# Attention 0 of a two-layer encoder: which engine makes the cosine products, the gated head outputs and the squares of the softmax sums

## The chip, the cores and the metric

The kernel runs on one core of a Trainium2 chip. Its five engines have a queue of instructions each and take them strictly in order: TensorE (PE in the profile, with its weight loads as PEld), VectorE (DVE), ScalarE (ACT), GpSimd (POOL) and SyncE (SP), which here only issues DMAs. They wait for each other through semaphores. The metric is the device time of one execution in microseconds; before the change the median of three runs is 1395.75 us (1395.17 to 1396.02).

Two memories matter. Tensors that work is done on lie in SBUF. Matmul results lie in PSUM, in eight banks of 128x512 fp32. A tile of PSUM is a bank here, or two for the scores.

## The reference, cut to what matters

Layer 0 is a differential attention with 8 heads of two 64-wide query/key components and 128-wide values, over 1024 positions; layer 1 is another attention that the change leaves alone.

```python
def _rope(x, positions):
    ...
    out = jnp.concatenate([x1 * cos - x2 * sin, x2 * cos + x1 * sin], axis=-1)

def _diff_attention(h, positions, w_in, ...):
    proj = h @ w_in
    q, k, v, z = jnp.split(proj, ...)
    q, k = _rope(q), _rope(k)
    ...
    def block(qb):
        sc = jnp.einsum('bqhcd,bkhcd->bhcqk', qb, k) * scale
        p = jax.nn.softmax(sc, axis=-1)
        p = p[:, :, 0] - lam * p[:, :, 1]
        return jnp.einsum('bhqk,bkhd->bqhd', p, v)
    ...
    o = _rmsnorm(o, subln_g) * (1.0 - lambda_init)
    o = o.reshape(b, s, DA_WIDTH) * jax.nn.silu(z)
    return o @ w_out
```

## The kernel before

The whole kernel is one straight program without loops on the chip; a framework resolves every dependency to semaphores and decides the order of each engine's queue when the program is built. `tc.keep_in_program_order` (through `in_turn`) and `tc.issue_after` (through `behind`) pin some instructions of the code to an order or behind another one.

A product in full precision is made of three matmuls on pairs of a high and a low part (`mm3`, lines 173 to 175). Making such a pair takes a cast on ScalarE (the high part, names that end in `h`) and a subtraction on VectorE or GpSimd (the low part, names that end in `l`).

**Attention 0** runs over heads 0 to 7, and per head over eight query tiles of 128 rows (`attn0`, `q_tile`). A query tile goes like this. For each of the two components c: four matmuls make the scores `s` (line 866, 128x1024, two banks; there are two such tiles), VectorE takes the row maximum `nm` (line 412), ScalarE the exponential `e` and its row sum (line 414). Then VectorE computes the ratio of the sums (`z`, lines 872 and 873) and combines the two components in one instruction (`e<-s,z,e`, line 874), which also sets the second score tile free. The combined tile is turned by eight transposes in two halves (`tr`, line 395; one bank); ScalarE makes the high part `pth` out of each half (line 397), VectorE the low part `ptl` (line 398), and only then is the one `tr` bank free for the next half. Every second query tile, matmuls with the values go into the bank `pv` (`Tail.pv`); after four query tiles, a half, the head's output 128x512 is complete there.

**Between these**, TensorE works on the stream (`stream0`): strips of k, q and the gate z of the next heads, 24 matmuls for each half of a strip, into the two `acc` banks (tables FILL0 and FILL7 say how many steps stand in which gap of a query tile). A finished half of a k or q strip goes to `rope`: ScalarE copies the bank to `rp_raw` (line 331 for k, 333 for q with its scale), four DMAs fetch the rotated rows into `rp_sw`, the cosine product `rp_r = rp_raw * cosT` is made (line 336), `rot` makes the sine product and adds it (lines 341 and 343, GpSimd), and `stack_k` / `stack_q` make the pairs `ks`, `qa` and `qb` for the scores: casts on ScalarE (356, 357, 364, 365), subtractions on GpSimd (358, 359, 366, 367), and DMAs for q. For head 0 VectorE does the cosine product, for heads 1 to 7 GpSimd (`eng`). `rp_raw`, `rp_sw` and `rp_r` share six buffers (tag `rp`).

**At the end of a half** `close` calls `head_out` and `subln`. `head_out` reads the `pv` bank twice on ScalarE: the squares `osq` (line 931) and `o`, scaled by the per-row constant `g8` (line 932). `subln` multiplies `o` by the gate `gz` on GpSimd (line 938); for the very last half (`late0`) VectorE does this (line 940). `rest`, some steps later, sums the squares with eight small matmuls into `ssq` (an `acc` bank, line 945) and makes the factor of each position out of `ssq` and the softmax sum `zz`: four VectorE instructions on 128x4 (lines 948 to 951), the power on GpSimd (`rq_y`, line 169) and a product with the guard `sl_f` (line 953). After a round trip through HBM that spreads the factor, `o` is scaled (line 908) and stored.

Of the kernel before, what the change touches and what calls it, by code (L numbers as in the profile page):

```python
# [15 lines left out]
AF = mybir.ActivationFunctionType  # L16
ALU = mybir.AluOpType
# [4 lines left out]
P = 128  # L22
# [5 lines left out]
NH = 8  # L28
QL = 384
KVL = 256  # L30
EPS = 1e-6
# [38 lines left out]
GUARD = 2.0 ** 40  # L70
FMAX = 3.4028e38
LAM0 = 0.8 - 0.6 * math.exp(-0.3 * 0)
SC0 = 64 ** -0.5
# [8 lines left out]
def trunk(ctx: ExitStack, tc: tile.TileContext, A, out):  # L82
    nc = tc.nc
    SP, PE, V, S, G = nc.sync, nc.tensor, nc.vector, nc.scalar, nc.gpsimd

    def pool(stack, name, bufs=1, side="left", space=None):
        kw = dict(name=name, bufs=bufs, reuse_waits="tile")
        if space is not None:
            kw["space"] = space
            if space == DRAM:  # L90
                kw.pop("reuse_waits")
        else:
            kw["side"] = side
        return stack.enter_context(tc.tile_pool(**kw))
# [49 lines left out]
    cosT = const.tile([P, T], F32, name="cosT")  # L144
# [14 lines left out]
    g8 = const.tile([P, 1], F32, name="g8")  # L159
# [20 lines left out]
    def behind(eng):  # L180

        return tc.issue_after(mk[eng]) if eng in mk else nullcontext()

    def in_turn(ins):

        return tc.keep_in_program_order(ins) if mk else ins
# [134 lines left out]
                self.count += 1  # L321
                side.tick()

    def rope(rp, acc, half, scale, eng=G, add=V):

        cs = slice(half * HF, half * HF + HF)
        raw = rp.tile([P, HF], F32, name="rp_raw", tag="rp", bufs=6)
        sw = rp.tile([P, HF], F32, name="rp_sw", tag="rp", bufs=6)
        r = rp.tile([P, HF], F32, name="rp_r", tag="rp", bufs=6)
        if scale == 1.0:  # L330
            S.copy(raw, acc)
        else:
            S.mul(raw, acc, scale)  # L333
        for q in range(4):
            SP.dma_start(sw[q * 32 : q * 32 + 32], raw[(q ^ 1) * 32 : (q ^ 1) * 32 + 32])
        r_ = eng.tensor_mul(r, raw, cosT[:, cs])  # L336
        if eng is G:
            in_turn(r_)

        def rot():  # L340
            in_turn(G.tensor_mul(sw, sw, sinT[:, cs]))
            if add is G:
                in_turn(G.tensor_add(r, r, sw))

        def fin():
            if add is not G:
                with behind("V"):
                    V.tensor_add(r, r, sw)
            return r

        return rot, fin

    def stack_k(t, r):

        with behind("S"):
            S.copy(t[0:64, 0, :], r[0:64])
            S.copy(t[64:128, 1, :], r[64:128])
        in_turn(G.tensor_sub(t[64:128, 0, :], r[0:64], f32v(t[0:64, 0, :])))
        in_turn(G.tensor_sub(t[0:64, 1, :], r[64:128], f32v(t[64:128, 1, :])))
# [144 lines left out]
    wp = pool(stW, "wp0", side="right")  # L504
# [261 lines left out]
    KS, QS, GZ = {}, {}, {}  # L766

    def k_done(h):
        def f(acc, half):
            rot, fin = rope(wp, acc, half, 1.0, *[G if h else V] * 2)  # L770

            def g():
                t = a0a.tile([P, 2, HF], F32R, name="ks", tag="ks", bufs=4)
                stack_k(t, r.pop() if r else fin())
                KS.setdefault(h, [None, None])[half] = t

            r = []
            sum_ = [lambda: r.append(fin()), None] if h else []
            side.add(*[None] * ROT, rot, *[None] * (DEF - 1 - ROT), *sum_, g)
        return f  # L780

    def q_done(h):
        def f(acc, half):
            rot, fin = rope(wp, acc, half, SC0, *[G if h else V] * 2)

            def g():
                qa = a0a.tile([P, 2, HF], F32R, name="qa", tag="qs", bufs=4)
                qb = a0a.tile([P, 2, HF], F32R, name="qb", tag="qs", bufs=4)
                stack_q(qa, qb, r.pop() if r else fin())
                QS.setdefault(h, [None, None])[half] = qa, qb  # L790

            r = []
            sum_ = [lambda: r.append(fin()), None] if 0 < h < 5 else []
            side.add(*[None] * ROT, rot, *[None] * (DEF - 1 - ROT - (h == NH - 1)), *sum_, g)
        return f
# [129 lines left out]

    ssq_at, rests, Y = [], [], []

    def head_out(o_, o, sq):


        S.activation(sq, o_, AF.Square, scale=1.0 / GUARD)
        S.mul(o, o_, g8[:, 0:1])

    def subln(o, sq, zz, half, h, dst):


        if dst is None:
            in_turn(G.tensor_mul(o, o, GZ[h][half]))
        else:
            V.tensor_mul(o, o, GZ[h][half])  # L940

        def rest():
            pt = Y[0] if dst is not None else ssq_at[0] if ssq_at else bank("acc", "ssq")
            for j in range(4):
                PE.matmul(pt[:, j : j + 1], sq[:, j * P : (j + 1) * P], ones[:, 0:1], start=True, stop=True)
            w = sm.tile([P, 4], F32, name="sl_w")
            fin = sm.tile([P, 4], F32, name="sl_f")
            V.tensor_mul(fin, zz, zz)
            V.scalar_tensor_tensor(out=w, in0=fin, scalar=P * EPS / GUARD ** 2, in1=pt[:, 0:4], op0=ALU.mult, op1=ALU.add)
            V.scalar_tensor_tensor(out=fin, in0=fin, scalar=FMAX / GUARD ** 2, in1=w, op0=ALU.mult, op1=ALU.is_ge)  # L950
            V.tensor_scalar(w, w, 3.0e38, None, op0=ALU.min)
            y = rsqrt(w, 4)
            in_turn(G.tensor_mul(y, y, fin))
            if dst is not None:
                return lambda: finish(o, y, 0, h, half, dst, None, sq)
            finish(o, y, 0, h, half, None, a0b, sq)

        if dst is None:
            (hooks if h < NH - 1 else rests).append(rest)
        else:  # L960
            return rest()
# [63 lines left out]
    def attn0(h, fills, extra=None, late=None):  # L1025

        def close(half, o_, zz):
            if late and half == 1:
                ctx_["late"] = late(o_, zz)
                return  # L1030
            o = a0b.tile([P, HF], F32, name="o", tag="o", bufs=2)
            sq = a0b.tile([P, HF], F32, name="osq", tag="osq", bufs=4)
            head_out(o_, o, sq)
            subln(o, sq, zz, half, h, None)

        ctx_ = dict(pool=a0b, l=0, h=h, open=lambda half: None, close=close)
        for qp in range(4):
            half = qp // 2
            if qp % 2 == 0:
                zz = first.pop(0) if first else sm.tile([P, 4], F32, name="zz")  # L1040
            for t in range(2):
                fl = fills(qp * 2 + t)

                def fill(i):
                    if fl[i]:
                        stream0.step(fl[i])

                def mid(c):
                    if c == 0:
                        fill(0)  # L1050
                        if tails[0]:
                            tails[0].turn(1)
                        fill(1)

                if first:
                    e0 = first.pop()
                else:
                    e0 = q_tile(h, half, (qp * 2 + t) % 4, zz, a0b, mid)
                    fill(2)
                    after_scores(fill, 3)  # L1060
                side.tick()
                tails[:] = [tails[1], Tail(qp, t, e0, zz, ctx_)]
                if extra:
                    extra(qp * 2 + t)
        if late:
            run_tails(lambda i: extra(8 + i))
            while hooks:
                hooks.pop(0)()
            return ctx_["late"]
# [293 lines left out]

    def late0(o_, zz):
        o, sq = k0["o"], k0["sq"]
        head_out(o_, o, sq)

        def f():
            fin = subln(o, sq, zz, 1, NH - 1, o)
            for n, t in ((2, k0["11"]), (3, sq), (4, k0["12"]), (5, k0["21"]), (6, o)):  # L1370
                sv0.kept[n][3] = t

            def g():
                fin()
                V.tensor_add(sq, k0["21"], o)
                V.tensor_sub(k0["21"], k0["11"], k0["21"])
                V.tensor_sub(k0["11"], sq, k0["11"])
                V.tensor_sub(k0["12"], k0["12"], k0["11"])

            return g  # L1380

        return f
# [141 lines left out]
    for n, rows, acc, f in ((3, 4, Z, 1), (4, 0, Z, 1), (5, 4, Y, 1), (6, 4, Y, 0)):  # L1524
# [5 lines left out]
        for i in range(4):  # L1530
# [24 lines left out]
            if i == 1 and n == 5:  # L1555
                raws = [[], []]
                with tc.issue_after(w6):
                    for k, (tag, nb) in enumerate((("wraw", 2), ("gz", 3))):
                        for f in range(2):
                            raw = wst.tile([P, HF], F32, name="wraw", tag=tag, bufs=nb)  # L1560
# [27 lines left out]
    wp = pool(stw, "wp1", side="right")  # L1588
# [197 lines left out]
    for h in range(2):  # L1786
        w = strip1(6 + h)
# [559 lines left out]
    for n, first, rows, acc, f, piece in ((3, True, 4, Z, 1, False), (4, False, 0, Z, 1, True), (5, False, 4, Y, 1, True)):  # L2347
        sp = sv.splits(n + 1)
        for i in range(4):
# [5 lines left out]
            add = add_to(rows + i, acc[i], f, piece=piece)  # L2355
# [8 lines left out]
    for tiles, a, b in LAST1:  # L2364
        acc = {i: bank("z", "oyb") if a else Y[i] for i in tiles}
# [87 lines left out]
```

## Time and profile before

| | before |
|---|---|
| median of three runs | 1395.75 us |
| the profiled execution, as timed | 1394.95 us |
| its span in the profile | 1393.2 us |
| granted TensorE clock, mean | 0.999 |
| attention 0 with the stream beside it | about 125 to 685 us of the span |

The profile is of one execution. What lies around its span (1394.95 less 1393.2) is 1.75 us. TensorE is called busy from a matmul's start to its modelled end; the "idle before" of a row, and the view of who waited for whom, show only the time in which it had nothing in flight. In the views, a row of a group reads: line, engine, operation, output<-inputs, shapes, count | busy us in total, mean ns of one | idle us of the engine before them, and what ended it. In the timeline, the two numbers ahead are the start and the length in us.

### The profile page before, as it was taken

To read this page: it belongs to the slowest core of one execution; us is meant where nothing else is said; L and a number is where in the kernel's file an instruction comes from. 1 tells how busy PE (TensorE), PEld (TensorE's weight loads), DVE (VectorE), ACT (ScalarE), POOL (GpSimd) and SP (SyncE) were. 2 spreads that over 40 slices of the span, in tenths; PEclk is the share of its full clock that TensorE was granted. 3 is DMA by queue.
4 is the path that set the end of the run, shared out by engine and by line. 5 is a ranking of instruction groups with operands and counts; after the bars stand their busy time and mean duration, and the time that the engine had idled before them with its cause. 6 is when DMAs were issued, how large, how long until landed. Compare 5 with 4: busy or idle time off the path is not lost.

```text
span 1393.2 us, 20695 instructions
## 1 busy us (share of the span) xinstructions
PE 1367.5 (98%) x7334; PEld 1144.7 (82%) x7334; DVE 928.3 (67%) x1313; ACT 740.9 (53%) x1339; POOL 753.1 (54%) x593
## 2 busy tenths in 40 slices
PE   9999999999999999999999999999999999999997
PEld 6788888888888887887887888888888888888886
DVE  7655777777666666668596976545656555555684
ACT  5532465656565555567648553335454544545554
POOL 5424374758686858575794233532141373834673
PEclk9999999999999999999999999999999999999999
DMA  9857644343444434526564246489443364667463
GB/s 342 263 177 244 201 110 141 100 144 105 149 127 144 128 121 122 151 61 212 182 219 167 68 137 212 137 282 286 125 105 119 102 201 136 193 221 215 145 245 121
DMA packets 149386, 232.06 MB, mean 167 GB/s; under 512 B 20641, under 2 KB 57633, under 8 KB 149282
## 3 DMA queue, kind: packets, MB, share of 16 engines
q1 hardware_dynamic: 149282, 230.74, 52.7%
q8 instruction: 58, 0.95, 0.3%
q14 instruction: 46, 0.38, 0.1%
HBM read 144.74 MB, written 61.81 MB: 148 GB/s over the span
## 4 chain that ended last, share of the span: by engine, by line
PE 79%; DVE 6%; DMA 5%; ACT 3%; POOL 3%; issue 2%; SPq 1%; POOLq 0%; ACTq 0%; DVEq 0%
PE s L2067 10%; PE acc L173 9%; PE acc L175 9%; PE acc L174 9%; PE tr L395 7%; PE s L866 7%; PE pv L173 4%; PE pv L174 4%; PE pv L175 4%; PE vps L173 2%; PE vps L174 1%; PE vps L175 1%; PE zacc L175 1%; PE zacc L173 1%; PE zacc L174 1%
## 5 line engine op out<-in xcount | busy, mean ns | idle before, releaser
L397 ACT CAST pth<-tr 128x512 fp32r<-128x512 f32 x256 | 150.3, 587 | 285.7 <-PE tr L395 280.8
L412 DVE TENSOR_REDUCE nm<-s 128x1 f32<-128x1024 f32 x192 | 233.8, 1218 | 79.8 <-PE s L866 70.9
L398 DVE TENSOR_TENSOR ptl<-tr,pth 128x512 fp32r<-128x512 f32 x256 | 176.1, 688 | 150.3 <-ACT pth L397 146.3
L219 POOL TENSOR_TENSOR wl<-wraw,wh 128x512 fp32r<-128x512 f32 (+2 forms) x77 | 98.8, 1284 | 208.4 <-ACT wh L218 176.3
L414 ACT ACTIVATE e<-s,nm 128x1024 f32<-128x1024 f32 x128 | 143.5, 1121 | 35.4 <-DVE nm L412 35.0
L395 PE MATMUL tr<-ident,e 128*128 128x128 f32 x1024 | 155.0, 273 | 4.1 <-DVE ptl L398 3.8
L395 PEld LDWEIGHTS tr<-ident,e 128*128 128x128 f32 x1024 | 120.7, 140 | 46.5 <-DVE ptl L398 24.1
L173 PE MATMUL acc<-h0h,wh 128*128 128x512 f32 x360 | 150.2, 417 | 0.0
L173 PE MATMUL pv<-pth,vt 128*128 128x256 f32 x512 | 147.5, 288 | 0.0
L174 PE MATMUL pv<-ptl,vt 128*128 128x256 f32 x512 | 145.6, 284 | 0.0
L175 PE MATMUL pv<-pth,vt 128*128 128x256 f32 x512 | 144.6, 282 | 0.0
L175 PE MATMUL acc<-h0h,wl 128*128 128x512 f32 x360 | 141.5, 393 | 0.0
L174 PE MATMUL acc<-h0l,wh 128*128 128x512 f32 x360 | 141.1, 392 | 0.0
L336 POOL TENSOR_TENSOR rp_r<-rp_raw,cosT 128x512 f32<-128x512 f32 x36 | 47.0, 1305 | 104.4 <-ACT rp_raw L333 52.9
L173 PEld LDWEIGHTS pv<-pth,vt 128*128 128x128 f32 x512 | 97.2, 190 | 2.9 <-ACT pth L397 0.2
L174 PEld LDWEIGHTS pv<-ptl,vt 128*128 128x128 f32 x512 | 97.4, 190 | 2.4
L175 PEld LDWEIGHTS pv<-pth,vt 128*128 128x128 f32 x512 | 97.3, 190 | 0.0
L1199 POOL TENSOR_TENSOR wol<-wol,woh 128x512 fp32r<-128x512 f32 x56 | 82.3, 1492 | 26.0 <-ACT woh L1198 24.4
L866 PE MATMUL s<-ks,qa 128*128 128x512 f32 x256 | 82.7, 403 | 4.4 <-DVE e L874 3.2
L874 DVE SCALAR_TENSOR_TENSOR e<-s,z,e 128x1024 f32<-128x1024 f32 x64 | 82.2, 1284 | 2.2
L866 PE MATMUL s<-ks,qb 128*128 128x512 f32 x256 | 79.8, 393 | 1.2 <-DMA qb<-qb 1.2
L175 PEld LDWEIGHTS acc<-h0h,wl 128*128 128x128 f32 x360 | 67.6, 188 | 15.1
(427 smaller groups left out, 3461.1 us busy)
## 6 DMA issues: line engine op xcount, KB each, us to landing
ada<-in_ada_ss SPq DMA_DIRECT2D x32, 512.0 KB, 5.9
wraw<-in_w_s SPq DMA_DIRECT2D x64, 256.0 KB, 2.8
vS<-v_hl SPq DMA_DIRECT2D x32, 512.0 KB, 5.9
vt<-vS SPq DMA_DIRECT2D x32, 512.0 KB, 4.9
wol<-tS SPq DMA_DIRECT2D x56, 256.0 KB, 5.2
tS<-ob SPq DMA_DIRECT2D x48, 256.0 KB, 2.0
rp_sw<-rp_raw SPq DMA_DIRECT2D x160, 64.0 KB, 2.0
bc_s<-bc_d SPq DMA_DIRECT2D x34, 256.0 KB, 4.2
```

Source lines behind the costliest of these rows:

```text
L173: PE.matmul(psum, ah, bh, start=first, stop=False, skip_group_check=skip)
L174: PE.matmul(psum, ah, bl, start=False, stop=False, skip_group_check=skip)
L175: mm3.last = PE.matmul(psum, al, bh, start=False, stop=last, skip_group_check=skip).ins
L219: sub = (V if pair_of else G).tensor_sub(l_[:, :n], raw[:, :n], f32v(h_[:, :n]))
L395: transpose_p.last = PE.transpose(tr[:, j, :], p[:, kt * P : (kt + 1) * P], ident).ins
L397: mk["S"] = S.copy(pth[kh][:, :, dst], tr).ins
L398: mk["V"] = V.tensor_sub(ptl[kh][:, :, dst], tr, f32v(pth[kh][:, :, dst])).ins
L412: mk["V"] = V.reduce_max(nm, s_ps, axis=AX.X, negate=True).ins
L414: mk["S"] = S.activation(e, s_ps, AF.Exp, bias=nm, scale=1.0, accum_out=zs).ins
L866: PE.matmul(s_ps[:, kc * HF : (kc + 1) * HF], src[:, c, ql], KS[h][kc][:, c, :], start=fst, stop=not fst)
L1199: sub = eng.tensor_sub(lo, raw, f32v(hi))
L2067: PE.matmul(s_ps[:, kc * HF : (kc + 1) * HF], lhs, rhs(kc), start=i == 0, stop=i == 4)
```

## The change

It does four things in attention 0.

- For k and q of heads 1 to 7, the cosine product is one VectorE instruction that reads the `acc` bank itself and applies the scale (`bank_`, 28 instructions). ScalarE's copy to `rp_raw` stays, since the rotation's DMAs read it.
- For all halves but the last, VectorE makes `o = pv * g8 * gz` in one instruction out of the `pv` bank (15 instructions); ScalarE's `o` and GpSimd's product with the gate go.
- The squares of `zz` that `rest` needs, with their constants, are made by ScalarE (two instructions on 128x4 for each half).
- VectorE's four instructions in `rest` become two, both of which read the `ssq` bank: the limit of 3.0e38 is applied to the bank's value as it is read, and the guard compares with the bank rather than with the sum.

```diff
-    def rope(rp, acc, half, scale, eng=G, add=V):
+    def rope(rp, acc, half, scale, eng=G, add=V, bank_=False):
...
-        r_ = eng.tensor_mul(r, raw, cosT[:, cs])
-        if eng is G:
-            in_turn(r_)
+        if bank_:
+            V.scalar_tensor_tensor(out=r, in0=acc, scalar=scale, in1=cosT[:, cs], op0=ALU.mult, op1=ALU.mult)
+        else:
+            r_ = eng.tensor_mul(r, raw, cosT[:, cs])
+            if eng is G:
+                in_turn(r_)
...
     def k_done(h):
         def f(acc, half):
-            rot, fin = rope(wp, acc, half, 1.0, *[G if h else V] * 2)
+            rot, fin = rope(wp, acc, half, 1.0, *[G if h else V] * 2, h > 0)
...
     def q_done(h):
         def f(acc, half):
-            rot, fin = rope(wp, acc, half, SC0, *[G if h else V] * 2)
+            rot, fin = rope(wp, acc, half, SC0, *[G if h else V] * 2, h > 0)
...
-    def head_out(o_, o, sq):
+    def head_out(o_, o, sq, h, half, late=False):
         S.activation(sq, o_, AF.Square, scale=1.0 / GUARD)
-        S.mul(o, o_, g8[:, 0:1])
+        if late:
+            S.mul(o, o_, g8[:, 0:1])
+        else:
+            V.scalar_tensor_tensor(out=o, in0=o_, scalar=g8[:, 0:1], in1=GZ[h][half], op0=ALU.mult, op1=ALU.mult)

     def subln(o, sq, zz, half, h, dst):
-        if dst is None:
-            in_turn(G.tensor_mul(o, o, GZ[h][half]))
-        else:
+        if dst is not None:
             V.tensor_mul(o, o, GZ[h][half])
...
-            V.tensor_mul(fin, zz, zz)
-            V.scalar_tensor_tensor(out=w, in0=fin, scalar=P * EPS / GUARD ** 2, in1=pt[:, 0:4], op0=ALU.mult, op1=ALU.add)
-            V.scalar_tensor_tensor(out=fin, in0=fin, scalar=FMAX / GUARD ** 2, in1=w, op0=ALU.mult, op1=ALU.is_ge)
-            V.tensor_scalar(w, w, 3.0e38, None, op0=ALU.min)
+            S.activation(w, zz, AF.Square, scale=math.sqrt(P * EPS) / GUARD)
+            S.activation(fin, zz, AF.Square, scale=1.0 / GUARD)
+            V.scalar_tensor_tensor(out=w, in0=pt[:, 0:4], scalar=3.0e38, in1=w, op0=ALU.min, op1=ALU.add)
+            V.scalar_tensor_tensor(out=fin, in0=fin, scalar=FMAX, in1=pt[:, 0:4], op0=ALU.mult, op1=ALU.is_ge)
             y = rsqrt(w, 4)
```

The calls follow: `close` passes `h, half`, and `late0` passes `NH - 1, 1, True`.

Three places show how the queues change. The first is GpSimd's queue while head 4's later query tiles run (460 to 471 us of the profile before). Before:

```order
L336 TENSOR_TENSOR rp_r<-rp_raw,cosT 128x512
L358 TENSOR_TENSOR ks<-rp_r,ks 64x512
L359 TENSOR_TENSOR ks<-rp_r,ks 64x512
L219 TENSOR_TENSOR wl<-wraw,wh 128x512
L938 TENSOR_TENSOR o<-o,gz 128x512
L1122 TENSOR_TENSOR ob_4304<-ot_4671,ob_4304 128x512
L1123 TENSOR_TENSOR ob_4305<-ob_4305,ot_4671 128x512
L341 TENSOR_TENSOR rp_sw<-rp_sw,sinT 128x512
L343 TENSOR_TENSOR rp_r<-rp_r,rp_sw 128x512
```

And now, at the same place (line numbers of the changed kernel are three to four higher):

```order
L361 TENSOR_TENSOR ks<-rp_r,ks 64x512
L362 TENSOR_TENSOR ks<-rp_r,ks 64x512
L219 TENSOR_TENSOR wl<-wraw,wh 128x512
L1126 TENSOR_TENSOR ob_4297<-ot_4663,ob_4297 128x512
L1127 TENSOR_TENSOR ob_4298<-ob_4298,ot_4663 128x512
L344 TENSOR_TENSOR rp_sw<-rp_sw,sinT 128x512
L346 TENSOR_TENSOR rp_r<-rp_r,rp_sw 128x512
```

Two of the nine are gone, the cosine product and the product with the gate; the rest stand in the order they had.

The second is VectorE's queue at the end of a half of head 4 (459 to 472 us of the profile before). Before:

```order
L874 SCALAR_TENSOR_TENSOR e<-s,z_4673,e 128x1024
L412 TENSOR_REDUCE nm<-s 128x1
L398 TENSOR_TENSOR ptl<-tr,pth 128x4x128
L412 TENSOR_REDUCE nm<-s 128x1
L398 TENSOR_TENSOR ptl<-tr,pth 128x4x128
L949 SCALAR_TENSOR_TENSOR sl_w<-sl_f,ssq 128x4
L950 SCALAR_TENSOR_TENSOR sl_f<-sl_f,sl_w 128x4
L872 RECIPROCAL z_4783<-z_4783 128x1
L951 TENSOR_SCALAR sl_w<-sl_w 128x4
L873 TENSOR_SCALAR z_4783<-z_4783,zz,neglam 128x1
```

And now:

```order
L877 SCALAR_TENSOR_TENSOR e<-s,z_4665,e 128x1024
L337 SCALAR_TENSOR_TENSOR rp_r<-acc,cosT 128x512
L938 SCALAR_TENSOR_TENSOR o<-pv,g_106,gz 128x512
L415 TENSOR_REDUCE nm<-s 128x1
L401 TENSOR_TENSOR ptl<-tr,pth 128x4x128
L415 TENSOR_REDUCE nm<-s 128x1
L401 TENSOR_TENSOR ptl<-tr,pth 128x4x128
L954 SCALAR_TENSOR_TENSOR sl_w<-ssq,sl_w 128x4
L955 SCALAR_TENSOR_TENSOR sl_f<-sl_f,ssq 128x4
L875 RECIPROCAL z_4774<-z_4774 128x1
L876 TENSOR_SCALAR z_4774<-z_4774,zz,neglam 128x1
```

The two new 128x512 instructions stand between the combination `e` and the next row maximum; the 128x4 instruction that stood between the two steps of `z` is gone. In the built program each of the two new ones waits for ScalarE's reading of the same bank (`rp_raw<-acc`, `osq<-pv`), and some `rp_r` also for GpSimd's last use of the buffer that they take.

The third is ScalarE's queue from the end of that half on (461 to 476 us of the profile before). Before:

```order
L931 ACTIVATE osq<-pv 128x512
L932 ACTIVATE o<-pv,g_106 128x512
L397 CAST pth<-tr 128x4x128
L414 ACTIVATE e,zz<-s,nm 128x1024
L397 CAST pth<-tr 128x4x128
L414 ACTIVATE s,z_4783<-s,nm 128x1024
L218 CAST wh<-wraw 128x512
L364 CAST qa<-rp_r 64x512
L365 CAST qa<-rp_r 64x512
L333 ACTIVATE rp_raw<-acc 128x512
L397 CAST pth<-tr 128x4x128
L414 ACTIVATE e,zz<-s,nm 128x1024
```

And now:

```order
L934 ACTIVATE osq<-pv 128x512
L400 CAST pth<-tr 128x4x128
L417 ACTIVATE e,zz<-s,nm 128x1024
L400 CAST pth<-tr 128x4x128
L417 ACTIVATE s,z_4774<-s,nm 128x1024
L218 CAST wh<-wraw 128x512
L367 CAST qa<-rp_r 64x512
L368 CAST qa<-rp_r 64x512
L333 ACTIVATE rp_raw<-acc 128x512
L400 CAST pth<-tr 128x4x128
L417 ACTIVATE e,zz<-s,nm 128x1024
L952 ACTIVATE sl_w<-zz 128x4
```

`o` is gone from ScalarE, and the first of the two small squares (`sl_w`, then `sl_f`) follows the exponential further down. The casts `qa`, which wait for GpSimd's `rp_r`, still stand ahead of a `pth` and an exponential.

More of the change, by code (lines that the diff above doesn't have):

```diff
@@ L1032, in close @@
             sq = a0b.tile([P, HF], F32, name="osq", tag="osq", bufs=4)
-            head_out(o_, o, sq)
+            head_out(o_, o, sq, h, half)
             subln(o, sq, zz, half, h, None)
@@ L1365, in late0 @@
         o, sq = k0["o"], k0["sq"]
-        head_out(o_, o, sq)
+        head_out(o_, o, sq, NH - 1, 1, True)
         def f():
```

## The prediction

> **What bounds the kernel now.** I read the page's table of engines first, then, for attention 0 alone, who TensorE waited for, and then the timeline around its longest waits.
>
> ```profile
> PE 1367.5 (98%) x7334; PEld 1144.7 (82%) x7334; DVE 928.3 (67%) x1313; ACT 740.9 (53%) x1339; POOL 753.1 (54%) x593
> ```
>
> TensorE is 98% busy, and the change touches none of its matmuls. So all that the change can win is TensorE's waiting in attention 0, and all that it can lose is new waiting there. The view of waits for TensorE from 125 to 640 us lists:
>
> ```profile
> PE s L866 <- DVE e L874: 1.9, 4, 0.7
> PE tr L395 <- DVE ptl L398: 1.3, 2, 0.9
> PE s L866 <- DMA qb<-qb: 1.2, 2, 0.7
> PE s L866 <- DMA qa<-qa: 0.9, 1, 0.9
> ```
>
> and from 640 to 685 us, where the stream has run out and nothing fills the gaps of the last head:
>
> ```profile
> PE tr L395 <- DVE ptl L398: 1.6, 3, 0.6
> PE s L866 <- DVE e L874: 1.3, 2, 1.0
> ```
>
> That is 5.3 us and 2.9 us, **8.2 us together: the ceiling** of what can be won by waits that this view sees (two more waits of the last head, of the output product, have nothing to do with the change). Who is behind them? The two windows show the load of the engines (columns: PE, PEld, DVE, ACT, POOL, each with its instructions):
>
> ```profile
> 125.00:640.00 515.00, 509.45 (x2815) 430.46 (x2813) 364.75 (x515) 294.63 (x520) 337.97 (x273) 1.00 0.46 136
> 640.00:685.00 45.00, 41.12 (x248) 33.67 (x247) 32.49 (x51) 30.31 (x56) 28.51 (x25) 1.00 0.55 171
> 405.00:475.00 70.00, 67.77 (x377) 56.86 (x375) 45.88 (x67) 40.15 (x71) 54.84 (x47) 1.00 0.48 147
> 195.00:265.00 70.00, 70.00 (x399) 60.18 (x398) 54.65 (x82) 41.16 (x74) 42.60 (x35) 1.00 0.43 122
> ```
>
> The granted clock is 1.00 throughout, so it explains nothing. From 195 to 265 us VectorE is busiest (54.65 of 70) and TensorE idles for nothing; from 405 to 475 us VectorE has 9 us less to do, GpSimd 12 us more, and TensorE loses 2.2 us. The waits go with **GpSimd's** load, though the list above names VectorE and DMAs. The timeline shows how, around 474 us:
>
> ```profile
> 451.87 1.29 POOL L359 TENSOR_TENSOR ks<-rp_r,ks 64x512 fp32r<-64x512 f32 x1
> ...
> 460.18 1.30 POOL L336 TENSOR_TENSOR rp_r<-rp_raw,cosT 128x512 f32<-128x512 f32 x1
> ...
> 465.53 1.30 POOL L938 TENSOR_TENSOR o<-o,gz 128x512 f32<-128x512 f32 x1
> 471.96 0.62 ACT L364 CAST qa<-rp_r 64x512 fp32r<-64x512 f32 x1 [2.23 <-POOL rp_r L343]
> 474.36 0.69 DVE L398 TENSOR_TENSOR ptl<-tr,pth 128x512 fp32r<-128x512 f32 x1 [0.94 <-ACT pth L397]
> 475.10 0.66 PE L395 MATMUL tr<-ident,e 128*128 128x128 f32 x4 [0.87 <-DVE ptl L398]
> ```
>
> Columns: start, length in us. GpSimd's rows follow each other almost without a gap from 451.87 us on. ScalarE stands in order before `qa` for 2.23 us until GpSimd's `rp_r` comes; the `pth` behind it is late, so `ptl`, so the one `tr` bank, and TensorE loses 0.87 us. Two of GpSimd's instructions ahead of that `rp_r` (460.18 and 465.53, 2.6 us) are among those that the change takes away. The DMA waits have the same root: the `qb` transfers follow GpSimd's subtractions.
>
> ```profile
> 407.14 1.29 POOL L367 TENSOR_TENSOR qb<-rp_r,qa 64x512 fp32r<-64x512 f32 x1
> 411.22 0.47 PE L866 MATMUL s<-ks,qb 128*128 128x512 f32 x1 [0.55 <-DMA qb<-qb]
> ```
>
> A third kind is VectorE's small 128x4 instruction, which takes 0.39 us on average and 1.22 us here, in the middle of the steps of `z`, while GpSimd is busy:
>
> ```profile
> 331.72 1.22 DVE L951 TENSOR_SCALAR sl_w<-sl_w 128x4 f32<-128x4 f32 x1
> 334.49 0.73 PE L866 MATMUL s<-ks,qa 128*128 128x512 f32 x2 [0.59 <-DVE e L874]
> ```
>
> **The change, part by part.** GpSimd and ScalarE lose these, in the groups from 125 to 685 us:
>
> ```profile
> L336 POOL TENSOR_TENSOR rp_r<-rp_raw,cosT 128x512 f32<-128x512 f32 x28 | 36.3, 1295 | 56.7 <-ACT rp_raw L331 51.2 <-ACT rp_raw L333 5.2
> L938 POOL TENSOR_TENSOR o<-o,gz 128x512 f32<-128x512 f32 x15 | 19.3, 1288 | 37.8 <-ACT o L932 37.8
> L932 ACT ACTIVATE o<-pv,g 128x512 f32<-128x512 f32 x15 | 10.3, 687 | 0.1
> ```
>
> GpSimd: 36.3 + 19.3 = 55.6 us less, of 366.5 in the two windows above. That is 15%, and by that share brings the stretch from 405 to 475 us from 54.8 to about 47 busy. ScalarE: 10.3 us less, and 32 small squares more. The trace has no square on 128x4; the nearest row is ScalarE's read of its accumulator on 128x1:
>
> ```profile
> L414 ACT ACTIVATION_READ_ACCUMULATOR s<-s,nm 128x1 f32 x64 | 13.0, 202 | 0.0
> ```
>
> I take 0.2 us, so +6.4 us; it can't cost less than nothing, and the square of a whole bank (0.60 us, the row of `osq` below) bounds it above at 19 us. ScalarE comes out about 4 us lighter (at the upper bound, 9 us heavier, of 325 busy in 560: still no bound).
>
> VectorE gains 43 instructions on 128x512 with one input in PSUM and loses small ones. The nearest row for the new ones is layer 1's own gated output, the same operation out of the same kind of bank:
>
> ```profile
> L2085 DVE SCALAR_TENSOR_TENSOR o<-pv,gz 128x512 f32<-128x512 f32 x15 | 10.4, 691 | 13.4 <-PE pv L175 13.0 <-POOL ob L1957 0.2 <-issue 0.2
> L948 DVE TENSOR_TENSOR sl_f<-zz 128x4 f32<-128x4 f32 x16 | 9.0, 565 | 0.0
> L950 DVE SCALAR_TENSOR_TENSOR sl_f<-sl_f,sl_w 128x4 f32<-128x4 f32 x15 | 6.3, 420 | 0.3
> L951 DVE TENSOR_SCALAR sl_w<-sl_w 128x4 f32<-128x4 f32 x15 | 5.8, 387 | 0.0
> L949 DVE SCALAR_TENSOR_TENSOR sl_w<-sl_f,ssq 128x4 f32<-128x4 f32 x14 | 2.1, 153 | 8.5 <-PE ssq L945 8.5
> ```
>
> 43 x 0.691 = +29.7 us. The three small ones without a PSUM input go, 9.0 + 6.3 + 5.8 = -21.1 us, and a second one that reads the bank comes, 16 x 0.153 = +2.4. Net **+11 us** on VectorE, 397 us busy before in the 560 (71% to 73%). Does it fit? VectorE's own waits from 125 to 640 us:
>
> ```profile
> DVE nm L412 <- PE s L866: 70.4, 55, 3.2
> DVE ptl L398 <- ACT pth L397: 33.5, 68, 1.0
> ```
>
> 104 us of slack stand exactly ahead of the two instructions next to which the new ones are put, 1.3 us on average in each of 55 places, and 0.49 us in each of 68. The head outputs fit best. At the place shown above, `e` ends at 460.68 us, and
>
> ```profile
> 461.36 0.60 ACT L931 ACTIVATE osq<-pv 128x512 f32<-128x512 f32 x1 [0.23 <-PE pv L175]
> 462.98 1.23 DVE L412 TENSOR_REDUCE nm<-s 128x1 f32<-128x1024 f32 x1 [2.29 <-PE s L866]
> ```
>
> `osq` is done at 461.96, `o` by 461.96 + 0.69 = 462.65, before the scores are there. Some `rp_r` stand where VectorE is back to back and push the next `ptl` or `nm` by up to 0.69 us; a query tile has slack for one of these as long as its neighbour waits. Also new: seven `ssq` groups wait for an `rp_r` on VectorE where they waited for ScalarE's copy; I count 0.3 us for all seven.
>
> The queues that nothing is taken from change little: TensorE has the same matmuls (some transposes stand one to three matmuls later, two `ssq` groups too), and SP the same DMAs, a few of them one or two places earlier or later.
>
> On the wait that the change adds: in the built program VectorE reads each bank only after ScalarE has, and the row at 462.98 says that this is hidden. The Trainium skill, "PSUM — Partial Sum Buffer", section "PSUM bank collisions raise a hardware error", says why it must be so: two engines may not read one bank and the same partitions at once. By that rule alone, with no slack counted, the 15 outputs would hold VectorE 15 x 0.60 us longer, and the sum would be +4 us, close to rival C; by the row it is -5 us, and I take the row.
>
> **Sum**, against the profiled execution (span 1393.2, as timed 1394.95). Of the 5.3 us before 640 us I expect 4.6 to go: all rest on GpSimd's queue or on the slow 128x4 instruction, but some `rp_r` will take a little back. In the last head VectorE is the bound; there VectorE loses small instructions of line 948 and 951:
>
> ```profile
> L948 DVE TENSOR_TENSOR sl_f<-zz 128x4 f32<-128x4 f32 x2 | 1.1, 532 | 0.0
> L951 DVE TENSOR_SCALAR sl_w<-sl_w 128x4 f32<-128x4 f32 x2 | 0.9, 434 | 0.0
> ```
>
> That is 2.0 us less, and one `o` more of 0.69 us; I take 0.7 of the remaining 1.3, as part of it lies beside waits. New waits cost 0.3. So -4.6 - 0.7 + 0.3 = **-5.0 us**: 1389.95 for the profiled execution. The median of the runs lies 0.8 us above that execution, so 1390.75; I say **1390.7 us**. Outside attention 0 the queues are as before, and the rest should only shift.
>
> **Rivals.**
>
> *A, transfers instead of the queue.* GpSimd, too, waits for the rotated rows:
>
> ```profile
> L341 POOL TENSOR_TENSOR rp_sw<-rp_sw,sinT 128x512 f32<-128x512 f32 x28 | 38.1, 1361 | 18.4 <-DMA rp_sw<-rp_raw 18.1
> ```
>
> Where those 18.1 us fall ahead of a late `rp_r`, an emptier queue doesn't bring it earlier, and ScalarE stands before `qa` as long as before. If that is so for half of the 4.6 us, -2.7 us are left: 1393.0, within the bound of no change.
>
> *B, no gain.* TensorE is 98% busy, and each wait taken away is replaced by one on VectorE, which is 11 us fuller: `PE s <- DVE e` grows as the others shrink. About 1395.5. The Trainium skill, "Perfetto Trace Analysis", section "Identifying the Most-Contended Engine", tells one to optimise the engine with the highest occupancy first, and to judge TensorE by its weight loads (82% here); by it GpSimd at 54% is the wrong engine, and the time stays at 1395.5. The windows above speak against it, since VectorE at 78% of its window cost TensorE nothing.
>
> *C, slower.* VectorE becomes the bound between `e` and `nm`: the new instruction holds up the row maximum or the combination, so the score banks come free late. Each place without slack costs up to 0.69 us. It breaks even where 5.0 / 0.69, some 7 of the 43, show on TensorE; with 15 of them it is +10.4 - 5.0 = +5.4 us, 1401. The slack ahead of `nm` speaks against it.
>
> *D, the change does less than it says.* The `rp_r` on VectorE wait for GpSimd's last use of their buffer, so GpSimd's backlog would stall VectorE instead. Against it: for the `rp_r` shown above, behind `e` at 460.68 us, that last use is the `ks` of 451.87, done at 453.16, over 7 us before, on the fuller queue. It would come out as B.
>
> **Chances.** A change is told from none here at 0.2%, 2.8 us: faster is below 1392.96, slower above 1398.54. The forecast and its neighbours from 1386 to 1392.9 hold 0.68; A 0.12, B with D 0.12, C 0.08. Faster 0.68, same 0.24, slower 0.08. The range goes from 1386.0 (the whole ceiling, and 1.5 us of short stalls that the view doesn't list) to 1397.0 (B, and the beginning of C).
>
> **What will show it.** Right: `PE s <- DMA qa` and `qb` vanish, ScalarE's wait for GpSimd's `rp_r` (2.23 us above) falls under 0.5 us, GpSimd is busy about 56 us less, and `rp_r` and `o` on VectorE take about 0.69 us. Wrong: `PE s <- DVE e` or `PE tr <- DVE ptl` grow beyond 3 us before 640 us (B, C), or the `qa` casts still wait for GpSimd with an `rp_sw` transfer ahead of it (A). The prediction falls if `o` or `rp_r` on VectorE take over 1 us, or stand waiting with scores ready behind them.

## The result, and the profile after

The changed kernel takes **1387.6 us** (median of six runs, 1386.7 to 1389.77); the kernel before, run beside it, 1396.27 us (1395.17 to 1397.74). The ratio is 0.9944, with a 95% interval of 0.9932 to 0.9956: 7.8 us faster (6.1 to 9.5); the two medians lie 8.7 us apart. Two more series of the same two kernels on other occasions gave 0.9944 (0.993 to 0.9957) and 0.9932 (0.9918 to 0.9946). The forecast was -5.0 us: the sign and the cause hold, the size was too small.

The profiled execution has a span of 1384.8 us, 8.4 less than before. Its table of engines (busy us, share of the span, instructions):

```profile
PE 1362.2 (98%) x7334; PEld 1145.7 (83%) x7334; DVE 940.0 (68%) x1324; ACT 736.5 (53%) x1356; POOL 701.6 (51%) x550
```

VectorE is 11.7 us fuller (+11 was forecast), ScalarE 4.4 us emptier (-4), GpSimd has 43 instructions and 51.5 us less. TensorE's share stands at 98% in both: the shares don't show the gain. The view of TensorE's waits from 125 to 640 us, and below the dots from 640 to 685 us (us in total, times, longest):

```profile
PE s L869 <- DVE e L877: 1.0, 2, 0.6
PE vps L173 <- DVE v_hl L378: 0.5, 1, 0.5
PE tr L398 <- DVE ptl L401: 0.4, 1, 0.4
...
PE s L869 <- DVE e L877: 1.2, 1, 1.2
PE tr L398 <- DVE ptl L401: 1.2, 2, 0.6
PE oy L175 <- POOL oal L1203: 0.5, 1, 0.5
```

5.3 us have become 1.9 before 640 us, and both DMA waits are gone. (The wait of `vps`, at 135 us, is listed for most of the experiments below too, with and without the change.) The windows, in the columns of the prediction:

```profile
125.00:640.00 515.00, 512.98 (x2857) 437.25 (x2856) 383.44 (x541) 294.16 (x541) 286.04 (x234) 1.00 0.45 136
640.00:685.00 45.00, 41.83 (x241) 34.35 (x240) 28.64 (x42) 29.74 (x61) 30.80 (x26) 1.00 0.64 208
405.00:475.00 70.00, 69.96 (x400) 59.89 (x399) 49.74 (x72) 41.81 (x77) 47.21 (x40) 1.00 0.51 153
```

In the same 515 us TensorE gets through 2857 matmuls instead of 2815, so the windows of after hold about 7 us more of the program. From 405 to 475 us it loses 0.04 us instead of 2.2: GpSimd is busy 47.2 us (the prediction's share gave "about 47"), VectorE 49.7.

The place that the prediction was built on, in the timeline of the changed kernel:

```profile
459.60 0.60 ACT L934 ACTIVATE osq<-pv 128x512 f32<-128x512 f32 x1 [0.29 <-PE pv L175]
460.23 0.75 DVE L938 SCALAR_TENSOR_TENSOR o<-pv,g,gz 128x512 f32<-128x512 f32 x1 [0.77 <-ACT osq L934]
461.21 1.23 DVE L415 TENSOR_REDUCE nm<-s 128x1 f32<-128x1024 f32 x1 [0.23 <-PE s L869]
...
466.37 1.28 POOL L346 TENSOR_TENSOR rp_r<-rp_r,rp_sw 128x512 f32<-128x512 f32 x1
467.85 0.62 ACT L367 CAST qa<-rp_r 64x512 fp32r<-64x512 f32 x1
470.07 0.59 ACT L400 CAST pth<-tr 128x512 fp32r<-128x512 f32 x1 [0.34 <-PE tr L398]
470.92 0.68 DVE L401 TENSOR_TENSOR ptl<-tr,pth 128x512 fp32r<-128x512 f32 x1
```

The sum `rp_r` is done at 467.65 us, and the cast `qa` starts at 467.85, where it started at 471.96 before. It no longer waits for the sum (its row has no bracket, where it had `[2.23 <-POOL rp_r L343]`) and is out of the way before `pth` is due, so `pth` waits for the transposes only. The new `o` waits 0.77 us for `osq`, and the row maximum behind it still waits 0.23 us for its scores. It starts 1.61 us after `osq` does, and before it was 1.62 (462.98 less 461.36): `o` costs nothing here. Over the whole of attention 0, in ScalarE's view of waits before, and then after:

```profile
ACT qa L364 <- POOL rp_r L343: 9.5, 6, 2.3
...
ACT qa L367 <- POOL rp_r L346: 1.7, 2, 0.9
```

### The profile page after: what moved, and what is told of

Its sections match the earlier page's. It is cut to its first block, busy times and chain, and to the rows that moved or that the text cites. A ratio compares the mean times of both kernels' runs of the same rounds, so it can differ in the third digit from the quotient of the medians.

```text
span 1384.8 us, 20703 instructions
## 1 busy us (share of the span) xinstructions
PE 1362.2 (98%) x7334; PEld 1145.7 (83%) x7334; DVE 940.0 (68%) x1324; ACT 736.5 (53%) x1356; POOL 701.6 (51%) x550
## 4 chain that ended last, share of the span: by engine, by line
PE 85%; DVE 6%; ACT 3%; DMA 3%; issue 2%; POOL 1%; SPq 1%; POOLq 0%; DVEq 0%; ACTq 0%
PE s L2071 10%; PE acc L173 9%; PE acc L175 9%; PE acc L174 9%; PE tr L398 8%; PE s L869 8%; PE pv L173 4%; PE pv L174 4%; PE pv L175 4%; DMA ada<-in_ada_ss 2%; PE oy L173 1%; PE oy L175 1%; PE oy L174 1%; PE zacc L174 1%; PE zacc L173 1%
## 5 line engine op out<-in xcount | busy, mean ns | idle before, releaser
L219 POOL TENSOR_TENSOR wl<-wraw,wh 128x512 fp32r<-128x512 f32 (+2 forms) x77 | 102.6, 1333 | 278.7 <-ACT wh L218 201.0
L174 PEld LDWEIGHTS acc<-h0l,wh 128*128 128x128 f32 x360 | 68.2, 189 | 9.2
```

The source lines that it names most:

```text
L174: PE.matmul(psum, ah, bl, start=False, stop=False, skip_group_check=skip)
L219: sub = (V if pair_of else G).tensor_sub(l_[:, :n], raw[:, :n], f32v(h_[:, :n]))
```

## The experiments

Each timing is against the kernel before, on the same chip. In us it is (ratio - 1) x the median of before there, 1397.9 to 1398.1, with the 95% interval. I call the prediction's explanation **Q**: what counts is how late GpSimd's queue comes to the sum `rp_r` for which ScalarE stands in order. Against it stand **S** (the shorter steps on 128x4), **A** (the `rp_sw` transfers), **P** (what helps is that the bank is read directly) and **K** (GpSimd's work costs because it disturbs VectorE's, wherever it stands in the queue). In the expectations of e1_rope to e4_busy, "Theory A" stands for another rival: that the gain comes from ScalarE, which loses `o`. I call that one **A'**.

| kernel | us against before | 95% | TensorE's waits listed, 125 to 640 | `qa` waits for `rp_r` |
|---|---|---|---|---|
| the kernel before | | | 5.3 | 9.5 |
| e4_busy | +1.7 | +0.4 to +2.8 | 6.1 | 10.2 |
| e10_ahead | -0.7 | -2.2 to +1.0 | 7.2 | 8.2 |
| e3_squares | -1.8 | -3.1 to -0.6 | 4.2 | 8.2 |
| e5_raw | -2.0 | -3.2 to -0.8 | 4.8 | 6.7 |
| e9_behind | -3.1 | -4.3 to -1.8 | 5.6 | 8.1 |
| e1_rope | -3.9 | -5.6 to -2.4 | 3.3 | 5.5 |
| e2_head | -4.2 | -5.7 to -2.7 | 4.2 | 5.5 |
| e6_relief | -6.3 | -8.0 to -4.5 | 3.2 | 2.8 |
| e7_no_squares | -6.4 | -8.2 to -4.8 | 3.1 | 2.4 |
| changed (e8_again) | -7.8 | -9.8 to -6.0 | 2.0 | 2.0 |
| e11_relief_sq | -8.1 | -9.9 to -6.3 | 1.2 | 2.4 |
| changed (e12_changed) | -9.5 | -11.5 to -7.5 | 1.4 | 1.9 |

The last two columns are from one profiled execution each; those of e4_busy (1400.9 us) and e6_relief (1395.0 us) took 1.9 and 3.3 us longer than their medians. A measure that needs no list of waits is the time between two matmuls that every kernel has: here the first of the scores after 330 us and the first after 640 us in the profile of before (the 185th and the 473rd of the kernel's score matmuls). Before, and then after:

```profile
330.91 0.71 PE L866 MATMUL s<-ks,qa 128*128 128x512 f32 x2
640.74 0.71 PE L866 MATMUL s<-ks,qa 128*128 128x512 f32 x2
...
332.10 0.71 PE L869 MATMUL s<-ks,qa 128*128 128x512 f32 x2
634.08 0.71 PE L869 MATMUL s<-ks,qa 128*128 128x512 f32 x2
```

309.8 us have become 302.0. That is 7.9 us less, and 7.0 and 7.4 less in e8_again and e12_changed: this stretch holds nearly the whole gain, and nothing is won ahead of it. In it e11_relief_sq wins 7.1 us, e7_no_squares 6.0, e6_relief 4.8, e1_rope 3.2, e2_head 2.9, e3_squares 2.4, e9_behind 1.0, e5_raw 0.6 and e10_ahead 0.0, and e4_busy loses 0.1.

**The parts alone.** e1_rope is the kernel before with the `bank_` lines of the diff only, e2_head with the new `head_out` and `subln` only, e3_squares with the four instructions of `rest` and ScalarE's two squares only.

> The kernel before with the cosine products alone moved to VectorE and the acc bank (28 instructions); head outputs and the 128x4 instructions as before. Theory Q (the time comes from GpSimd's queue, which is shorter by these 36.3 us of 55.6): about two thirds of the whole gain of 8 us or a little more, -4 to -6 us, and the waits of TensorE for the qa and qb transfers gone. Theory S (the time comes from VectorE's slow 128x4 instructions in the steps of z): no more than -1 us. Theory A (it comes from ScalarE, which loses o): nothing, 0 +- 1 us.

> The kernel before with the gated head outputs alone moved to VectorE and the pv bank (15 instructions; 19.3 us less on GpSimd, 10.3 us less on ScalarE). Theory Q: about a third, -2 to -3 us. Theory S: 0 +- 1 us. Theory A: nearly all of the gain, -6 us or more.

> The kernel before with the squares of the softmax sums alone moved to ScalarE and the guard by the bank (VectorE loses about 21 us of small instructions and gets 2.4). Theory Q: at most -1.5 us, from the two places where a slow 128x4 instruction stood ahead of e (332 and 541 us). Theory S: -4 us or more. Theory A: 0 or slower, since ScalarE gets 6.4 us more.

-3.9, -4.2 and -1.8 us; the parts add up to -9.9, more than the whole. e1_rope lies at the edge of Q's -4 to -6. For e2_head it is more than Q said and less than A', and e3_squares falls between Q and S, its interval reaching Q. A' falls as the account of the whole: e1_rope wins while `o` is still on ScalarE. The first two cut ScalarE's wait from 9.5 to 5.5 us, with GpSimd 34 and 17 us emptier. What Q said of the transfers missed: in e1_rope the waits for `qb` (1.2 us) and `qa` (0.3) are still there, where the full change has none:

```profile
PE s L869 <- DMA qb<-qb: 1.2, 2, 0.7
...
ACT qa L367 <- POOL rp_r L346: 5.5, 6, 1.8
```

**The queue filled again.** e4_busy is the changed kernel, in which GpSimd makes the 43 old products all the same, into a buffer that nobody reads:

```diff
             V.scalar_tensor_tensor(out=r, in0=acc, scalar=scale, in1=cosT[:, cs], op0=ALU.mult, op1=ALU.mult)
+            in_turn(G.tensor_mul(scr, raw, cosT[:, cs]))
...
+            in_turn(G.tensor_mul(scr, o, GZ[h][half]))
```

> The changed kernel, but GpSimd still does its 28 cosine products and 15 products with the gate, into a buffer that nobody reads, at their old places in its queue; VectorE and ScalarE as in the changed kernel. Theory Q: most of the gain is lost again, 1393 to 1396 us, and ScalarE waits for GpSimd's rp_r ahead of qa by 1 to 2 us in several places again. Theories S and A: it stays at 1387 to 1389 us.

The whole gain is gone, and 1.7 us more. Its table of engines, ScalarE's wait, and TensorE's waits that came back:

```profile
PE 1368.5 (98%) x7334; PEld 1147.4 (82%) x7334; DVE 941.7 (67%) x1324; ACT 736.4 (53%) x1356; POOL 755.7 (54%) x593
...
ACT qa L369 <- POOL rp_r L348: 10.2, 6, 2.5
...
PE tr L400 <- DVE ptl L403: 2.0, 3, 1.0
...
PE s L871 <- DMA qb<-qb: 1.0, 2, 0.5
PE s L871 <- DMA qa<-qa: 0.8, 1, 0.8
```

S falls: the short steps are all there, and nothing is left of the gain. A falls as the account of the whole: the transfers are those of the changed kernel. So does A', as ScalarE is as light as there (736.4 and 736.5 us). K has little to stand on: with GpSimd's 43 products back, VectorE's 1324 instructions take 941.7 us, and 938.9 to 941.8 in three profiles of the changed kernel. What came back are waits, not longer instructions.

That it is 1.7 us slower than before, and not just as slow, seems to belong to the experiment. In its profile TensorE loses 2.5 us in the last head, from the 473rd to the last of attention 0's score matmuls. There GpSimd's unread product has to wait for VectorE (before, it waited for ScalarE's `o`), and holds up what the output product needs, which is part of the loss:

```profile
665.93 1.29 POOL L941 TENSOR_TENSOR scr<-o,gz 128x512 bf16<-128x512 f32 x1 [3.45 <-DVE sl_w L957]
669.73 0.63 PE L175 MATMUL oy<-wol,oah 128*128 128x512 f32 x1 [1.06 <-POOL wol L1206]
```

In e10_ahead below, where the products wait for nothing, that stretch takes no longer than before (0.3 us less).

**The same products elsewhere in the queue.** e10_ahead and e9_behind make 43 equal products that wait for nothing, the first in the old places, the second behind the pairs of a half and behind the guard:

```diff
+                if h:
+                    in_turn(G.tensor_mul(scr, cosT[:, 0:HF], sinT[:, 0:HF]))
...
             in_turn(G.tensor_mul(y, y, fin))
+            if dst is None:
+                in_turn(G.tensor_mul(scr, cosT[:, 0:HF], sinT[:, 0:HF]))
```

> The changed kernel with 43 products on GpSimd that nobody reads (cosT times sinT, 128x512, into a spare bf16 buffer), 28 of them behind the two subtractions that make the pair of a k or q half, 15 behind the product with the guard: the same work as before the change, but never between a rotated half and the sum rp_r that ScalarE waits for in that half. Theory Q (what stands ahead of rp_r in GpSimd's queue): less is lost than with the products in their old places; a half's product still delays whatever comes next, so I expect -3 to -6 us against the kernel before, and a wait of ScalarE for rp_r between 3 and 7 us. Theory K (GpSimd's work costs by itself, wherever it stands, because it disturbs VectorE's instructions on SBUF): as e10_ahead, within 1.5 us of it.

> The same 43 products as e9_behind (same operands, which wait for nothing), in the old places: where the cosine product and the gate product stood. Theories Q and K both: the gain is gone as in e4_busy (1.7 us slower than before), so -1 to +2.5 us against the kernel before; a wait of ScalarE for rp_r of 8 to 11 us.

e10_ahead loses the gain as expected; e9_behind keeps 3.1 us of it. The two ratios lie 0.0017 apart, and their intervals (0.9969 to 0.9987, and 0.9984 to 1.0007) overlap a little; by the two matmuls above, e9_behind is only 1.0 us shorter than e10_ahead. So the place seems to count, but less than I thought: most of the gain goes wherever the products stand. These timings alone don't exclude K, which said within 1.5 us. VectorE's busy time speaks against it once more: 941.7 us in e9_behind and 940.8 in e10_ahead, as in the changed kernel. ScalarE's wait was misjudged:

```profile
ACT qa L368 <- POOL rp_r L347: 8.1, 8, 1.7
ACT ks L360 <- POOL rp_r L347: 6.1, 5, 1.9
```

14 us, where 3 to 7 were expected: behind one half is ahead of the next. That this kernel, with more such waiting than e10_ahead (8.2 and 2.4 us), is still the faster says that the sum of ScalarE's waits is no price. That only a wait which also holds up a `pth` that is due costs anything is my reading; no run shows it.

**The copy instead of the bank.** e5_raw is the kernel before with `V.tensor_mul(r, raw, cosT[:, cs])` on VectorE for the 28 products.

> The kernel before, with the 28 cosine products of heads 1 to 7 moved to VectorE, but made as before out of the copy in SBUF (rp_raw times cosT) and not out of the bank; all else as before. It takes the same 36 us off GpSimd's queue as e1_rope, which was 3.9 us faster than the kernel before, without reading the bank. Theory Q (GpSimd's queue is what counts): most of that gain stays, -1 to -4 us; it is smaller than e1_rope's by what the two inputs in SBUF cost, since four VectorE products of this form for head 0 in the kernel before took 959 ns on average (679 to 1781) instead of 0.69 us, 28 x 0.27 = 7.6 us more on VectorE, of which most lies in its slack. Rival P (what helps is that the bank is read directly): no gain, or slower, within 1 us of the kernel before or above.

-2.0 us, half of e1_rope's 3.9, where Q said most of it. P falls as the whole account, since moving the product helps without reading the bank, but a share of e1_rope's gain may come from the bank: the intervals overlap, and between the two matmuls above e5_raw wins 0.6 us where e1_rope wins 3.2. The group of these products on VectorE:

```profile
L336 DVE TENSOR_TENSOR rp_r<-rp_raw,cosT 128x512 f32<-128x512 f32 x28 | 24.5, 875 | 6.8 <-ACT rp_raw L331 3.2 <-ACT rp_raw L333 1.4 <-POOL ob L1112 0.9
```

**The relief alone.** e6_relief takes the 43 products away and puts nothing in their place; e11_relief_sq adds the new `rest`.

```diff
+        if not none_:
             r_ = eng.tensor_mul(r, raw, cosT[:, cs])
...
-                in_turn(G.tensor_add(r, r, sw))
+                in_turn(G.tensor_add(r, raw if none_ else r, sw))
...
-        if dst is None:
-            in_turn(G.tensor_mul(o, o, GZ[h][half]))
-        else:
+        if dst is not None:
```

> The kernel before, with the 28 cosine products of heads 1 to 7 and the 15 gate products on GpSimd left out and nothing put in their place: the rotation's sum takes rp_raw in place of the cosine product, and the head outputs of the first 15 halves are not gated, so this part of the computation is missing. It is the relief of GpSimd's queue alone, 55 us, without the new work of VectorE. Theory Q: the change's gain (7.8 us) and the cost of its new work on VectorE and ScalarE (e4_busy was 1.7 us slower than before) add up, so about -9.5 us, -8 to -11. Theory S (the shorter 128x4 steps and the squares count for more): at most -5. Theory A (the transfers of rp_sw set the end): -3 or less, as the sum still waits for rp_sw.

> e6_relief (cosine and gate products of attention 0 left out, the same parts of the computation missing) with the squares on ScalarE and the guard by the bank added: the changed kernel without the 43 new instructions of VectorE, but with ScalarE's 15 scaled outputs. If VectorE's new work costs nothing behind its waits: as the changed kernel, -7.3 to -8.5 us. If it costs the 1.7 us by which e4_busy was slower: -9 to -10.

-6.3 us: less than Q's -8 to -11, so adding e4_busy's loss to the change's gain was wrong. (S's "at most -5" lies inside the interval too; it is e4_busy that speaks against S.) It is nevertheless what e7_no_squares gives, which is the changed kernel with the old `rest`:

> The changed kernel with the old four VectorE instructions on 128x4 in the factor's steps and no squares on ScalarE, so the cosine products and the gated head outputs together. If the parts add up, the changed kernel's -7.8 less e3_squares' -1.8: about -6 us, -5 to -7. Theory Q adds that the slow 128x4 instructions get shorter here too, since GpSimd is less busy, so the squares are worth less in the changed kernel than alone: -6.5 to -7.8. Theory S: -3 or less.

> The changed kernel as it is, on the same chip as the three others, so that they can be compared with it: -7 to -8.5 us by every theory.

> The changed kernel as it is, beside the three others on the same chip: -7 to -8.5 us.

-6.3 beside -6.4 us, and with the new `rest` -8.1 (e11_relief_sq) beside -7.8 and -9.5: the 43 new instructions of VectorE cost nothing that these runs can tell. e6_relief and e11_relief_sq leave ScalarE its 15 `o`s and come out like e7_no_squares and the changed kernel, so ScalarE's relief is worth nothing here that can be told either. The -9.5 lies outside the -7 to -8.5 that was expected of the same kernel, and 1.7 us from e8_again: two series can differ by that much, and smaller differences between rows of different occasions say little. e7_no_squares fits the sum of the parts, and with its interval (-8.2 to -4.8) Q's addition (-6.5 to -7.8) as well.

## Why the prediction was right, and where its sizes were off

- **The cause.** GpSimd's queue, named from one stretch of the timeline, is shown by e4_busy and e10_ahead (filled again, no gain) and e6_relief (emptied and nothing else, most of the gain; the limit on 128x4 got shorter there too, see the last section). Which of the waits behind that queue count, and for how much, is shown for the place at 474 us only.
- **The ceiling and "Of the 5.3 us before 640 us I expect 4.6 to go".** This term was mis-sized, because a listed wait costs more than its number: TensorE counts as busy to a matmul's modelled end, which lies beyond the usual start of the next. At 474 us the last matmul ahead of the wait was, before, and then the same two after:

```profile
473.83 0.40 PE L175 MATMUL acc<-h0h,wl 128*128 128x512 f32 x1
...
471.95 0.39 PE L175 MATMUL acc<-h0h,wl 128*128 128x512 f32 x1
472.18 0.60 PE L398 MATMUL tr<-ident,e 128*128 128x128 f32 x4
```

  From the start of `acc` to that of `tr` (475.10 in the prediction's row) it was 1.27 us, and is 0.23: 1.04 us won, where the wait is listed with 0.87. For the whole stretch I took the same matmuls in both profiles: the 536th of the kernel starts at 125.07 us before and 124.95 after, the 3349th at 640.07 and 633.41. So 6.5 us were won in place of 4.6. Of this, 5.0 lie in gaps over 0.25 us longer than the median for the same pair of products: there were ten, worth 7.0 us (nine of them are the listed 5.3 us), and three are left, worth 2.0. The other 1.5 come from short ones that the view doesn't list, for which the range had 1.5 us but the sum nothing.

  Two of the three gaps that are left lie ahead of 171 us. From 125 to 170 us the one profile of before is 0.6 to 2.4 us shorter than every other profile, with or without the change; there that profile was a good one, and the change lost nothing. Of the nine listed waits, one is left behind 171 us (0.45 us, 0.65 before).
- **The last head, -0.7.** From there to the 3594th matmul (685.03 before, 677.53 after) 44.97 us became 44.12: -0.85, and -0.4 and -0.85 in the two other profiles of the changed kernel. The size held; that it comes from the small instructions, no run shows.
- **New waits, +0.3.** None shows on TensorE. -6.5 - 0.85 = -7.4 of the 8.4 us between the spans; most of the rest (0.85) lies behind 685 us, where nothing was changed. In the two other profiles of the changed kernel that part is 0.1 and 1.0 us longer than before, so it differs from execution to execution.
- **VectorE.** The new instructions, and the small ones of `rest`:

```profile
L337 DVE SCALAR_TENSOR_TENSOR rp_r<-acc,cosT 128x512 f32<-128x512 f32 x28 | 19.2, 685 | 4.3 <-ACT rp_raw L331 3.0 <-POOL ob L1116 0.6 <-ACT rp_raw L333 0.2
L938 DVE SCALAR_TENSOR_TENSOR o<-pv,g,gz 128x512 f32<-128x512 f32 x15 | 11.2, 750 | 8.1 <-ACT osq L934 8.0
L954 DVE SCALAR_TENSOR_TENSOR sl_w<-ssq,sl_w 128x4 f32<-128x4 f32 x14 | 2.2, 159 | 7.8 <-PE ssq L949 7.8
L955 DVE SCALAR_TENSOR_TENSOR sl_f<-sl_f,ssq 128x4 f32<-128x4 f32 x14 | 2.1, 148 | 0.0
```

  30.4 us for the 43, where 29.7 were forecast. The slack ahead of `nm`, 70.4 us before, paid for them:

```profile
DVE nm L415 <- PE s L869: 42.8, 50, 2.4
...
DVE o L938 <- ACT osq L934: 8.0, 9, 1.4
```

- **The banks' rule.** VectorE does wait for ScalarE's reading of `pv`, 8.0 us in 9 places, as the Trainium skill ("PSUM — Partial Sum Buffer", "PSUM bank collisions raise a hardware error") makes one expect. Its `rp_r` waits another 3.2 us for `rp_raw`. But it waits in time that it had. The sum by the row held, not the +4 us by the rule alone.
- **ScalarE's squares.** 0.2 us was the estimate, and the two groups have means of 206 and 193 ns:

```profile
L952 ACT ACTIVATE sl_w<-zz 128x4 f32<-128x4 f32 x16 | 3.3, 206 | 0.4
L953 ACT ACTIVATE sl_f<-zz 128x4 f32<-128x4 f32 x16 | 3.1, 193 | 0.0
```

- **Rival A.** GpSimd does wait longer for the transfers now, which changes nothing, as it is early enough:

```profile
POOL rp_sw L344 <- DMA rp_sw<-rp_raw: 26.8, 10, 4.7
```

- **Rivals B, C, D.** `PE s <- DVE e` and `PE tr <- DVE ptl` didn't grow before 640 us (1.0 and 0.4). VectorE's `rp_r` waited 0.6 us for GpSimd in all, at one place (D):

```profile
319.31 0.69 DVE L337 SCALAR_TENSOR_TENSOR rp_r<-acc,cosT 128x512 f32<-128x512 f32 x1 [0.58 <-POOL ob L1116]
319.92 1.22 DVE L415 TENSOR_REDUCE nm<-s 128x1 f32<-128x1024 f32 x1
```

  There the matmuls of the scores that `nm` takes had ended at 318.50 us, while `rp_r` still waited. The prediction had named this as a sign against itself; it came once, and TensorE lists no wait there. The Trainium skill ("Perfetto Trace Analysis", "Identifying the Most-Contended Engine") has one optimise the engine with the highest occupancy first. The gain came from taking work off GpSimd, which was at 54%, with VectorE at 67% and TensorE at 98%.
- **Of the other signs,** two were off. ScalarE's wait for `rp_r` is gone at the place named, but two such waits are left, the longest of 0.9 us and not under 0.5. And GpSimd is 51.5 us less busy, not about 56. The 43 products are gone; others got longer, above all `wl` (before, then after, the whole span):

```profile
L219 POOL TENSOR_TENSOR wl<-wraw,wh 128x512 fp32r<-128x512 f32 (+2 forms) x77 | 98.8, 1284 | 208.4 <-ACT wh L218 176.3 <-PE acc L1771 11.8 <-DMA bc_s<-bc_d 7.0
...
L219 POOL TENSOR_TENSOR wl<-wraw,wh 128x512 fp32r<-128x512 f32 (+2 forms) x77 | 102.6, 1333 | 278.7 <-ACT wh L218 201.0 <-issue 44.1 <-PE acc L1775 11.8
```

Still open: which of the changed kernel's places the squares' 1 to 2 us come from, and why 15 gate products are worth as much as 28 cosine products. e2_head also takes 10.3 us off ScalarE, and no run separates the two in that kernel. No variant beat the changed kernel clear of the noise; what is still listed for TensorE in attention 0 is about 2 us before 640.

## What to carry to other kernels

An engine at half load can still cost the one at 98% something: look where it is back to back, who stands in order for its result, and what is queued behind the one who stands. Moving work was free here, where the receiving engine had waits directly beside most of the places. And price a vanishing wait by the distance between starts, not by the idle time listed: here ten gaps, nine of them listed at 5.3 us, were worth 7.0, and the short ones, listed nowhere, gave another 1.5. And compare the same matmuls of two profiles, not the same times.

## What the runs showed of the hardware

VectorE's product of two SBUF inputs took 875 ns on average (e5_raw), and out of the bank 685 ns in e1_rope, for the same 128x512. Half of the 28 in e5_raw took 693 ns or less, and the longest 1800, so a few make the mean. The limit on 128x4, from SBUF to SBUF, took half the time where GpSimd had 43 products less to do (the group of that line before, and in e6_relief):

```profile
L951 DVE TENSOR_SCALAR sl_w<-sl_w 128x4 f32<-128x4 f32 x15 | 5.8, 387 | 0.0
...
L950 DVE TENSOR_SCALAR sl_w<-sl_w 128x4 f32<-128x4 f32 x15 | 2.7, 179 | 0.0
```

The Trainium skill, "SBUF — State Buffer", section "Who interferes with whom", says that a VectorE instruction with two SBUF inputs contends with a GpSimd instruction that reads SBUF, and one with at most one doesn't, outside its 2-port modes. The rows agree: with the bank as one input, `sl_w` and `sl_f` stayed at 158 and 148 ns, and `rp_r` at 684, in e4_busy, where GpSimd was as full as before. The limit on 128x4 has one input in SBUF and was slower beside a full GpSimd all the same; whether it ran in such a mode, no run shows.
